# A hybrid pooling, SSD and gated-DeltaNet layer with mixture of experts: backward tokens stored reversed, inverses begun from 16-blocks and merged by matmuls

## The chip, the cores and the metric

The kernel runs on one core of one Trainium2 chip. A core has a matrix engine (PE, with its weight loads PEld), a vector engine (DVE), a scalar engine (ACT), a general engine (POOL) and a queue engine that issues transfers (SP). Each works through its own list of instructions in order, and they meet through semaphores. The metric is device microseconds of one execution, the median over runs.

## The reference

The program is one layer of a diffusion backbone over 2048 latent tokens and 256 context tokens of 1024 channels. After a modulated norm, one projection feeds three head groups: pooling, a bidirectional SSD scan and a bidirectional gated DeltaNet (GDN) scan. An output projection, a router and a mixture of 16 experts follow. The change is in GDN, which has 6 heads of 64 channels and works in chunks of 64 tokens, 36 chunks in each direction:

```python
def gdn_chunked(q, k, v, g, beta, s0):
    ...
    decay = jnp.exp(jnp.where(lower, gc[..., :, None] - gc[..., None, :], -jnp.inf))
    kb = kc * bc[..., None]
    xm = jnp.where(strict, jnp.einsum('bnhik,bnhjk->bnhij', kb, kc) * decay, 0.0)
    tm = lax.linalg.triangular_solve(xm + eye, jnp.broadcast_to(eye, xm.shape), ...)
    u = jnp.einsum('bnhij,bnhjv->bnhiv', tm, vc * bc[..., None])
    w = jnp.einsum('bnhij,bnhjk->bnhik', tm, kb * jnp.exp(gc)[..., None])
    attn = jnp.einsum('bnhik,bnhjk->bnhij', qc, kc) * decay
    ...
    def step(s, inp):
        v_new = u_i - jnp.einsum('bhlk,bhkv->bhlv', w_i, s)
        o_i = jnp.einsum('bhlk,bhkv->bhlv', qg_i, s) + jnp.einsum('bhij,bhjv->bhiv', a_i, v_new)
        s = s * ge_i[..., None, None] + jnp.einsum('bhlk,bhlv->bhkv', ke_i, v_new)
        return s, o_i
```

The backward direction is the same on tokens flipped in time, and its output is flipped back and added before a norm and a gate.

## The kernel before

The program has phases. **A** (lines 169 to 591) projects all tokens; `conv_block` also convolves blocks of 128 channels and writes them to DRAM, queries and keys by channel in `qk_d` (line 468), keys and values by token in `kv_d` (line 495). **Scalars** (593 to 781) makes the decay rows. **B** (790 to 1355) holds the scans. **C** (1361 to 1481) is the output projection and the router, **D** and **E** are the experts.

Phase B is where the change lies. A Python loop (line 1270) emits, for each step n, `gdn_prep(n)`, the SSD tiles of that step, `NINV` pieces of the batched inverses, then the recurrence `gdn_chain(nxt)`, which follows `LAG` steps behind, and from time to time two tiles of the output projection that need pooling and SSD alone (`fill_0`, "fills" below). The emitted order is not the executed one: a scheduler orders each engine's list by the priorities that `tc.high_priority` gives (the chain has the highest), and by the buffers of the pools.

- `gdn_prep(n)` multiplies keys by keys and queries for the chunk of both directions (lines 1019 and 1022). Forward and backward lie in one token order, so each direction's stationary operand `kz` is loaded apart, with zeros in the other half of its 128 rows (lines 1008 to 1010). DVE scales the products by the decay into `xk` and `XQ` (line 1025). `XQ` is written to `xq_d` (line 1027) and read again by `gdn_kv` (line 995). ACT copies the diagonal 32-blocks into a batch of 32 (line 1043).
- `gdn_inv(b)` inverts 32 blocks of 32x32 in each group of 32 partitions by forward substitution: 31 columns, two DVE operations each (lines 1071 and 1073), between transposes (1064, 1065, 1079 to 1082). `merge(n)` makes the 64-block inverse of a step from two 32-blocks in two rounds of matmuls (lines 1092 and 1093, then 1098 and 1099) with ACT copies between them.
- `gdn_chain(n)` is the recurrence: state times keys (line 1133), residual `gR` (1135), inverse times residual (1151), `vn` (1153, 1154), update (1159), new state `gS` (1163); for latent steps also the output from the state (1144) and from `vn` (1169). `gdn_out` (1180) finishes a chunk when both directions have reached it.

An fp32 matmul of the source is two MATMUL instructions in the trace, so the 12 of six heads and two directions are 24. A matmul's tile of the array is written rows*columns, as 64*32.

Of the kernel before, what the change touches and what calls it, by code (L numbers as in the profile page):

```python
# [42 lines left out]
FSR = P + H * P  # L43
RB = 1
HPO = 2000
NXQ = 2
SF = 0.9
LAG = 9
NINV = 7
NEND = 1  # L50
NPS = 3
# [19 lines left out]
def tile_kernel(ctx, tc, a, out, stop=None, dump=None):  # L71
# [34 lines left out]
    def rsqrt_newton(eng, y, x, tmp, n):  # L106
        """y = x ** -0.5 on [P, w] tiles (y and tmp F32)"""
# [6 lines left out]
    def rsqrt_bits(pool, x, shape, eng, name):  # L114
        """x ** -0.5 from the exponent's halving and Newton's iteration"""
# [21 lines left out]
    # ---------------------------------------------------------------- constants  # L137
# [7 lines left out]
    # ---------------------------------------------------------------- DRAM scratch  # L145
# [4 lines left out]
    qk_d = dram("qk_d", [6, P, TT])  # L150
    kv_d = dram("kv_d", [TT, 2 * HW])
    xb_d = dram("xb_d", [TT, HW + 256])
# [4 lines left out]
    gx_d = dram("gx_d", [216, P])  # L157
# [3 lines left out]
    xq_d = dram("xq_d", [NSTEP - CSTEP, P, HW])  # L161
# [6 lines left out]
    # ---------------------------------------------------------------- phase A: projections  # L168
# [10 lines left out]

    stA = ExitStack()  # L180
# [5 lines left out]
    def low(k, lo, hi):  # L186
        """low parts of hT's tokens lo .. hi - 1"""
# [9 lines left out]
    with tc.tile_pool(name="t1", bufs=1, side="right") as pool:  # L197
# [8 lines left out]
        # the modulation's weights lie where hT comes to lie, the first tokens where its last low parts do  # L206
# [10 lines left out]
        def raw_T(tiles):  # L217
            """the normed tokens of two tiles, transposed"""
# [96 lines left out]
        # rows of the small products that give the exponents: two of each head's, then those of the free tokens;  # L315
        # what of them is the same for all steps
# [75 lines left out]
        for r in range(2):  # L392
            S.dma_start(dap(ab_d, (TC + r) * 24, [[ROWS * 24, GW], [48, NT], [1, 24]]), ab[r * 64:(r + 1) * 64, NCT:, :])

# [18 lines left out]
    def proj(w, n):  # L413
        """block n of tokens: 0..3 lat, 4 ctx"""
# [26 lines left out]
    def conv_block(kind, cb):  # L441
        """kind 'q' (columns of qkv, column-major tokens) or 'x' (xbc)"""
# [12 lines left out]
        for n in (4, 0, 1, 2, 3):  # L455
# [11 lines left out]
            if kind == "q" and cb < 6:  # L467
                SY.dma_start(dap(qk_d, cb * P * TT + tok0, [[TT, P], [1, w]]), av)
# [32 lines left out]
    def ada_chunks(n):  # L501
        """128 columns at a time of m2 .. m5"""
# [69 lines left out]
    for blk in BLOCKS.split():  # L572
# [4 lines left out]
        if blk == "q6":  # L577
# [3 lines left out]
            for t, c in ((lnk, 0), (ssq, 6)):  # L581
                SY.dma_start(dap(ss_d, c, [[12, P], [P * 12, 18], [1, 6]]), t)
        conv_block(kind, cb)
        ada_chunks(2)
# [8 lines left out]
    # ---------------------------------------------------------------- scalars of the scans  # L593
# [21 lines left out]
    with tc.tile_pool(name="scal", bufs=1, side="right", reuse_waits="tile") as sp:  # L615
# [11 lines left out]
        def halves(name, lo, hi, anti=False):  # L627
# [3 lines left out]
            c0, c1 = (64, 0) if anti else (0, 64)  # L631
            V.tensor_copy(m[0:64, c0:c0 + 64], lo[0:64, 0:64])
            V.tensor_copy(m[64:128, c1:c1 + 64], hi[64:128, 64:128])
            return m

        g_inc = halves("g_inc", m_ge, m_le)
        g_str = halves("g_str", m_lt, m_gt)
        g_all = halves("g_all", ones, ones, anti=True)
# [24 lines left out]
        for h, d in ((0, 1), (64, 0)):  # L663
# [10 lines left out]
        # log(1 + e) = log(u) * e / (u - 1), or e where u is 1  # L674
# [10 lines left out]
        def put_rows(src, n, puts):  # L685
            """DRAM rows of 128 tokens from the n * 108 columns of src"""
# [15 lines left out]
        # GDN  # L702
# [31 lines left out]
        put_rows(fl(g2[:, 0]), 2, lambda t: SY.dma_start(dap(gx_d, 0, [[P, 108], [108 * P, 2], [1, P]]), t))  # L734
# [4 lines left out]
        # SSD  # L739
# [50 lines left out]
    # ---------------------------------------------------------------- phase B: scans  # L790
# [16 lines left out]
    SY.dma_start(dsk, dap(a["ssd_d"], 0, [[0, P], [1, 6]]))  # L807
    identb = gt_("identb", [P, P], 1, BF)
    V.tensor_copy(identb, ident)
    # NEG where the scan's order forbids a pair of tokens  # L810
# [18 lines left out]
    # rows 32-95 add NEG to the pairs that the order forbids  # L829
    for g in gPQt:  # L830
        for r in (slice(32, 64), slice(64, 96)):
            for s in range(2):
                V.tensor_scalar(g[r, s, 0:64], jp[r, 0:64], -32.0, NEG, op0=OP.is_lt, op1=OP.mult)
# [4 lines left out]
    # ---- SSD  # L838
# [97 lines left out]
    # ---- GDN: in token-major tiles rows 0-63 are the backward scan's chunk, rows 64-127 the forward scan's;  # L936
    # in channel-major tiles and in the state it is the other way round
# [860 lines left out]
```

## Time and profile before

| | us |
|---|---|
| runs, median of 3 (lowest to highest) | 2398.49 (2390.59 to 2404.88) |
| profiled execution: span from its first to its last instruction (no other time of it is given) | 2391.4 |
| busy in it: PE, DVE, ACT, POOL | 2084.4, 1733.0, 1077.5, 834.8 |
| phase B, from 782 to 1460 | 678 |

The busy time of an engine is the time in which at least one of its instructions ran; PE's matmuls overlap, so sums over groups of lines exceed it. The granted clock is the share of TensorE's full clock that it had over a stretch. The DMA share is the mean busy share of the 16 transfer engines.

### The profile page before, as it was taken

Reading aid. Unit: us, or ns where it says so; the run is one execution under the profiler, and the core shown is the slowest. Engines: PE = TensorE matmul, PEld = TensorE weight load, DVE = VectorE, ACT = ScalarE, POOL = GpSimd, SP = SyncE. Lnnn points to the kernel's source line nnn. Section 1 sums busy time; section 2 is a strip of 40 time slices with the busy share of each in tenths; the row PEclk is TensorE's granted clock in tenths of the full one; section 3 lists DMA queues with packets and bytes.
Section 4 is the critical chain, followed back from the end, with each engine's and each line's share of the span. In section 5 each row is a group of like instructions: output and inputs, shape, how many; then the busy total and the mean of one; then the engine's idle time right before and its main releaser. Section 6 shows DMA issues by size and latency. Waiting matters only on the chain. (4 is left out here: it accounts for less than half of the span.)

```text
span 2391.4 us, 44610 instructions
## 1 busy us (share of the span) xinstructions
PE 2084.4 (87%) x16769; PEld 1797.7 (75%) x16769; DVE 1733.0 (72%) x3635; ACT 1077.5 (45%) x2136; POOL 834.8 (35%) x755
## 2 busy tenths in 40 slices
PE   5789999999988667999988797996499999988886
PEld 2778888888867556778777676884489999978775
DVE  7666776877754698998898765546656766788876
ACT  5443333443314345556654442554144444455552
POOL 1002333355331435454453442445221111133453
PEclk8899999999989778999997898998699999998998
DMA  7433234433323997999876675655268778788883
GB/s 236 123 92 97 80 116 122 135 102 94 94 66 80 233 245 188 217 217 221 191 191 165 163 179 192 209 199 182 84 193 243 218 227 229 222 268 284 293 272 141
DMA packets 418033, 424.72 MB, mean 178 GB/s; under 512 B 151987, under 2 KB 312602, under 8 KB 416794
## 3 DMA queue, kind: packets, MB, share of 16 engines
q1 hardware_dynamic: 398106, 368.33, 53.6%
q0 software_dynamic: 14816, 50.03, 8.0%
q10 hardware_dynamic: 4896, 3.51, 0.5%
q8 instruction: 133, 2.18, 0.4%
q14 instruction: 82, 0.67, 0.1%
HBM read 309.55 MB, written 112.22 MB: 176 GB/s over the span
## 5 line engine op out<-in xcount | busy, mean ns | idle before, releaser
L1641 ACT ACTIVATE wh<-wr 128x1024 fp32r<-128x1024 f32 x192 | 202.1, 1056 | 255.5 <-PE pgate L134 74.7
L133 PE MATMUL pj<-hTh,wh 128*128 128x512 f32 (+1 forms) x800 | 308.1, 385 | 5.3 <-ACT wh L192 4.4
L461 DVE SCALAR_TENSOR_TENSOR acc<-u,PV,acc 128x512 f32<-128x512 f32 (+1 forms) x320 | 281.9, 930 | 39.1 <-ACT acc L459 21.1
L135 PE MATMUL pj<-hTh,wl 128*128 128x512 f32 (+1 forms) x800 | 306.9, 384 | 3.5 <-DVE wl L193 3.5
L134 PE MATMUL pj<-hTl,wh 128*128 128x512 f32 (+1 forms) x800 | 309.0, 386 | 0.0
L1643 DVE TENSOR_TENSOR wl<-wr,wh 128x1024 fp32r<-128x1024 f32 x176 | 221.3, 1263 | 104.8 <-ACT wh L1641 101.4
L133 PEld LDWEIGHTS pj<-hTh,wh 128*128 128x128 f32 x800 | 153.7, 192 | 37.4 <-ACT wh L192 4.7
L135 PEld LDWEIGHTS pj<-hTh,wl 128*128 128x128 f32 x800 | 153.3, 192 | 34.5 <-DVE wl L193 4.2
L134 PEld LDWEIGHTS pj<-hTl,wh 128*128 128x128 f32 x800 | 153.4, 192 | 29.6 <-issue 0.7
L506 POOL TENSOR_TENSOR aw<-aw,sc 128x1024 f32<-128x1024 f32 x32 | 68.4, 2139 | 251.1 <-DMA aw<-in_ada_w_dram 233.0
L134 PE MATMUL pgate<-xel,wh 128*128 128x256 f32 x512 | 151.0, 295 | 3.0 <-DVE xel L193 3.0
L133 PE MATMUL pgate<-xeh,wh 128*128 128x256 f32 x512 | 149.3, 292 | 3.6 <-ACT xeh L192 3.5
L135 PE MATMUL pgate<-xeh,wl 128*128 128x256 f32 x512 | 150.3, 294 | 0.0
L133 PE MATMUL pup<-xeh,wh 128*128 128x256 f32 x512 | 148.6, 290 | 0.0
L135 PE MATMUL pup<-xeh,wl 128*128 128x256 f32 x512 | 146.9, 287 | 0.0
L134 PE MATMUL pup<-xel,wh 128*128 128x256 f32 x512 | 146.7, 287 | 0.0
L1740 POOL DMA_INDIRECT x_d<-ye,idx x30 | 48.9, 1631 | 206.0 <-DVE ye L1734 128.6
L1071 DVE TENSOR_TENSOR tmpb<-Wb,Vb 128x31 f32<-128x31 f32 (+15 forms) x217 | 107.7, 496 | 5.7 <-POOL Vb L1063 1.9
L1073 DVE TENSOR_TENSOR Vb<-Vb,tmpb 128x31 f32<-128x31 f32 (+15 forms) x217 | 108.7, 501 | 3.7
L133 PE MATMUL pdown<-wh,hh 128*128 128x512 f32 x256 | 104.6, 408 | 7.6 <-DVE ye L1734 3.3
L133 PEld LDWEIGHTS pgate<-xeh,wh 128*128 128x128 f32 x512 | 101.4, 198 | 5.0 <-ACT xeh L192 4.6
L134 PEld LDWEIGHTS pgate<-xel,wh 128*128 128x128 f32 x512 | 101.6, 198 | 3.2 <-DVE xel L193 3.2
(581 smaller groups left out, 5927.8 us busy)
## 6 DMA issues: line engine op xcount, KB each, us to landing
wr<-in_exp_w_gate_dram SPq DMA_DIRECT2D x64, 512.0 KB
wr<-in_exp_w_up_dram SPq DMA_DIRECT2D x64, 512.0 KB
wr<-in_exp_w_down_dram SPq DMA_DIRECT2D x64, 512.0 KB
aw<-in_ada_w_dram SPq DMA_DIRECT2D x32, 512.0 KB
kv<-kv_d SPq DMA_DIRECT2D x72, 192.0 KB
xb<-xb_d SPq DMA_DIRECT2D x35, 320.0 KB
wr<-in_w_in_dram SPq DMA_DIRECT2D x21, 512.0 KB
aw<-in_ada_w_dram SPq DMA_DIRECT2D x8, 1024.0 KB
```

The costliest lines, as they stand in the source:

```text
L133: TE.matmul(o, lh, rh, start=start, stop=False, **kw)
L134: TE.matmul(o, lh, rl, start=False, stop=False, **kw)
L135: TE.matmul(o, ll, rh, start=False, stop=stop, **kw)
L461: V.scalar_tensor_tensor(av, u[:, s0 - 2 + i:s0 - 2 + i + w], cw[:, i, cb:cb + 1], av, op0=OP.mult, op1=OP.add)
L506: G.tensor_tensor(w, w, sc2[:, :, 0:1].to_broadcast([P, KT, P]), op=OP.mult)
L1071: V.tensor_tensor(t, W[:, c + 1:, c:c + 1].to_broadcast([P, nr, ncl]), N[:, c:c + 1, :ncl].to_broadcast([P, nr, ncl]), op=OP.mult)
L1073: V.tensor_tensor(N[:, c + 1:, :ncl], N[:, c + 1:, :ncl], t, op=OP.subtract)
L1641: S.activation(wh, w, AF.Copy)
L1643: (G if nw[0] <= 16 else V).tensor_tensor(wl, w, wh.bitcast(F32), op=OP.subtract)
L1740: G.indirect_dma_start(out=x2_d, out_offset=rows_of(e, h), in_=ys[h], in_offset=None, compute_op=OP.bypass if late else OP.add)
```

## The change

Backward tokens are stored in reversed order, so that both directions have the same lower-triangular form: rows 0 to 63 of every tile are the forward scan, rows 64 to 127 the backward one. Then:

- `qk_d` gets one 6 KB row for a channel, a pair of chunks and a direction, written twice by `conv_block`, the second time from a copy that ACT reverses. Copies of `kv_d`, `ab_d` and `ss_d` with reversed tokens are made by DRAM-to-DRAM transfers (`reverse`).
- The matmuls of prep and chain contract 64 rows, and the two directions alternate; `kz` and its zeros are gone. Query products stay in `xk` (9 buffers) and do not go through `xq_d`. `vn` and `gS` are one operation for both directions in place of two.
- Inverses start from 16-blocks: 15 columns of at most 128 elements in place of 31 of at most 256. `merge` makes 32-blocks and then 64-blocks in five rounds of matmuls, three of them in 32*32 tiles.
- `gdn_out` turns and adds the other direction's output by a matmul with `turned`, `go_d` is written in chunks and read by four transfers in place of one.
- `LAG` 9 to 7, `NINV` 7 to 6, PSUM banks of SSD (`NPS`) 3 to 2, of `pm` 1 to 2.

```diff
+QKR = 2 * H * P
-LAG = 9
-NINV = 7
+LAG = 7
+NINV = 6
-NPS = 3
+NPS = 2
...
+    def reverse(dst, src, w, c, n):
+        for k0, k in ((CSTEP, NSTEP - CSTEP), (0, CSTEP)):
+            o = k0 * 64 * w + c
+            SY.dma_start(dap(dst, o, [[64 * w, k], [w, 64], [1, n]]), dap(src, o + 63 * w, [[64 * w, k], [-w, 64], [1, n]]))
...
             if kind == "q" and cb < 6:
-                SY.dma_start(dap(qk_d, cb * P * TT + tok0, [[TT, P], [1, w]]), av)
+                rv = ct("st", 512, 3)
+                S.activation(rv[:, :w], av[:, ::-1], AF.Copy)
+                for src, m in ((av, t0), (rv[:, :w], 18 + (0 if n == 4 else NSTEP // 2 + CSTEP // 2 - t0 - nt))):
+                    for h in range(2):
+                        SY.dma_start(dap(qk_d, m * 64 * QKR + (1 - cb // 3) * H * P + (2 * (cb % 3) + h) * P,
+                                         [[QKR, 64], [64 * QKR, nt], [1, P]]), src[64 * h:64 * h + 64])
...
     def load_kq(m, name, bufs):
-        n = 2 * m
-        kq = (gt_ if name == "kq" else lt)(name, [P, 2, H, 2, HD], bufs)
-        for i in range(2 if n >= CSTEP else 1):
-            o = (0 if i else HW) * TT
-            SY.dma_start(kq[0:64, i].rearrange("p h s t -> p h (s t)"),
-                         dap(qk_d, o + n * 64, [[TT, 64], [64 * TT, H], [1, P]]))
-            for s in range(2):
-                SY.dma_start(kq[64:128, i, :, s, :], dap(qk_d, o + chunk_b(n + s) * 64, [[TT, 64], [64 * TT, H], [1, 64]]))
+        kq = (gt_ if name == "kq" else lt)(name, [P, 2, H, P], bufs)
+        for d in range(2):
+            SY.dma_start(kq[DS[d]].rearrange("p a b c -> p (a b c)"),
+                         dap(qk_d, (18 * d + m) * 64 * QKR, [[QKR, 64], [1, QKR]]))
         return kq
...
-            for i in range(3):
-                h = 3 * hg + i
-                TE.matmul(pg[64:128, i, 0:nq, :], kz[:, 0, h, :], kq[:, 0:nq, h, s, :], start=True, stop=True)
             for i in range(3):
                 h = 3 * hg + i
-                TE.matmul(pg[0:64, i, 0:nq, :], kz[:, 1, h, :], kq[:, 0:nq, h, s, :], start=True, stop=True)
+                for d in range(2):
+                    TE.matmul(pg[DS[d], i, 0:nq, :], of(kq, d, 0, h, s), of(kq, d, slice(0, nq), h, s), start=True,
+                              stop=True)
...
         def column(c):
-            W, N = T_["W"], T_["N"]
-            nr, ncl = 31 - c, c + 1
+            W, N = diagonal(T_["W"]), diagonal(T_["N"])
+            nr, ncl = 15 - c, c + 1
...
             for h in range(h0, h1):
-                c = n * H + S0 + h - 32 * b
-                TE.matmul(pm[96:128, 0, h, :], xo[64:128, h, :], yt[64:128, c, :], start=True, stop=True)
-                TE.matmul(pm[0:32, 0, h, :], xo[0:64, h, :], yt[0:64, c, :], start=True, stop=True)
-            for p0 in (96, 0):
-                S.activation(qt[p0:p0 + 32, h0:h1], pm[p0:p0 + 32, 0, h0:h1], AF.Copy)
+                for q in range(4):
+                    c = 32 * (q % 2)
+                    TE.matmul(pa[QS[q], h, :], xk[QS[q], h, 0, c:c + 32], yt[QS[q], c0 + h, 0:16], start=True, stop=True)
+            V.scalar_tensor_tensor(a16[:, hh, 0:16], pa[:, hh, :], upper[:, 0:1],
+                                   eyes[:, 0:1, 0:16].to_broadcast([P, w, 16]), op0=OP.mult, op1=OP.add)
             for h in range(h0, h1):
...
+                for q in range(4):
+                    TE.matmul(py[QS[q], 0, h, :], a16[QS[q], h, :], yd[QS[q], c0 + h, :], start=True, stop=True)
+            for h in range(h0, h1):
+                for q in range(4):
+                    TE.matmul(py[QS[q], 1, h, :], yd[QS[q], c0 + h, :], a16[QS[q], h, :], start=True, stop=True)
...
+            for h in range(h0, h1):
+                for d in range(2):
+                    TE.matmul(pm[DS[d], 0, h, :], xk[QS[2 * d], h, 0, :], y2[QS[2 * d], 1, h, :], start=True, stop=True)
+            S.activation(a32[:, hh, 0:32], pm[:, 0, hh, :], AF.Copy, scale=-1.0)
...
             ks = bank(pb, "pc", [H, HD], 1)
-            for d, (o, i) in enumerate(fb):
-                for h in range(H):
-                    TE.matmul(ks[o, h, :], kqg[:, 0, h, s, :], st[:, d, h, :], start=True, stop=True)
+            for h, d in hd:
+                TE.matmul(ks[DS[d], h, :], of(kqg, d, 0, h, s), st[DS[d], h, :], start=True, stop=True)
...
-        V.tensor_tensor(h3(oe), po, h3(oe), op=OP.add)
+        TE.matmul(po.rearrange("p h d -> p (h d)"), turned, oe, start=False, stop=True, skip_group_check=True)
```

The order of the lists shows three of its places. On PE, around one late step of the recurrence; names are tiles, `pc` the chain's bank, `pm` the merges' bank, `pp` prep's, and a row gives the line, the tiles and the moving operand's shape. Before:

```order
L1005 MATMUL pp<-gPQ_6141 128x384
L1019 MATMUL pp<-kq,kz_6202 64x128 x3
L1133 MATMUL pc<-gS_6225,kqg 64x64 x12
L1144 MATMUL po<-gS_6225,kqg 64x64 x12
...
L1151 MATMUL pc<-gR,Yt_6207 64x64 x12
L1022 MATMUL pp<-kq,kz_6202 64x128
...
L1092 MATMUL pm<-YT,XO_6189 32x32
L1093 MATMUL pm<-YT,XO_6189 32x32
```

and in the change:

```order
L1177 MATMUL pc<-gR,Yt_6367 64x64 x12
L947 MATMUL ps<-xb,sE 128x64 x5
L1121 MATMUL pm<-YT,xk 32x16 x9
L1183 MATMUL pc<-vn,ke 64x64 x12
L1191 MATMUL po<-vn,xk 64x64 x12
L1207 MATMUL po<-oe_13850,turned 128x384
L1121 MATMUL pm<-YT,xk 32x16 x4
L1167 MATMUL pc<-gS,kqg 64x64 x12
```

A merge's rounds are now cut into pieces that stand between the chain's groups, and every change of the tile's shape is one more. Counted over phase B, from the first `gPQ` matmul to the last output of `vn`, the shape changes 416 times before and 782 times now, and the source's matmuls go from 4058 to 6649.

On DVE, the last columns of a batch of inverses (`tmpb` is the product, `Vb` the inverse) before:

```order
L1071 TENSOR_TENSOR tmpb<-Wb,Vb 128x112
L1073 TENSOR_TENSOR Vb<-Vb,tmpb 128x4x28
L1071 TENSOR_TENSOR tmpb<-Wb,Vb 128x87
```

and in the change:

```order
L1095 TENSOR_TENSOR tmpb<-Wb,Vb 128x110
L1097 TENSOR_TENSOR Vb<-Vb,tmpb 128x2x5x11
L1095 TENSOR_TENSOR tmpb<-Wb,Vb 128x96
L886 TENSOR_TENSOR S_7759<-ssg,ps 128x384
L1097 TENSOR_TENSOR Vb<-Vb,tmpb 128x2x4x12
```

Each column still has two operations, on two 16-blocks at once, and a batch has 15 columns.

On SP, the loads of a pair of steps before (`kz`, the products' round trip, and rows of 64 and 128 tokens):

```order
L966 DMA kqg<-qk_d 64x6x64 x2
L963 DMA kqg<-qk_d 64x6x128
L966 DMA kqg<-qk_d 64x6x64 x2
L991 DMA kv<-kv_d 64x768
L1010 DMA kz_6202<-qk_d 64x6x64
...
L1027 DMA xq_d<-XQ 128x384
```

and in the change:

```order
L1030 DMA kv<-kvr_d 64x768
L1004 DMA kq<-qk_d 64x1536 x2
L1217 DMA go_d<-oe 64x384 x2
```

Six issues for the keys and queries of a pair have become two, and `kz`, `xq_d` and `XQr` have gone.

## Rows read from the trace of the kernel before

**Rows 1.** Busy time by stretch: length, PE, PEld, DVE, ACT, POOL; clock, DMA share, GB/s.
```profile
300.00:400.00 100.00, 100.00 (x521) 84.14 (x520) 68.29 (x93) 37.20 (x57) 36.28 (x28) 1.00 0.42 124
782.00:876.00 94.00, 58.11 (x390) 45.41 (x390) 71.49 (x135) 38.82 (x105) 40.35 (x54) 0.70 1.00 246
1000.00:1200.00 200.00, 184.12 (x2651) 158.95 (x2653) 179.37 (x357) 122.69 (x358) 96.53 (x103) 0.95 0.89 210
1200.00:1460.00 260.00, 217.26 (x3023) 190.34 (x3023) 198.80 (x431) 118.54 (x357) 116.96 (x179) 0.89 0.66 170
1500.00:1600.00 100.00, 100.00 (x593) 82.69 (x592) 49.34 (x153) 50.41 (x127) 47.43 (x20) 1.00 0.56 196
```

**Rows 2.** The same view over the whole of phase B.
```profile
782.00:1460.00 678.00, 566.72 (x7596) 487.68 (x7596) 563.01 (x1148) 351.85 (x1028) 308.32 (x394) 0.89 0.81 199
```

**Rows 3.** Groups of PE's instructions in phase B: busy us, mean ns, idle before.
```profile
L1019 PE MATMUL pp<-kq,kz 128*64 128x128 f32 (+1 forms) x432 | 64.2, 297 | 7.2 <-ACT gE L1007 3.9 <-PE pp L1005 1.7 <-DMA kq<-qk_d 0.6
L1169 PE MATMUL po<-vn,XQr 128*64 128x64 f32 x768 | 56.7, 230 | 1.6 <-ACT vn L1153 1.4
L1159 PE MATMUL pc<-vn,ke 128*64 128x64 f32 x840 | 50.5, 229 | 0.9 <-ACT vn L1154 0.9
L907 PE MATMUL ps<-S,cb 128*128 128x192 f32 x64 | 14.0, 344 | 0.0
```

**Rows 4.** Timeline of PE: start us, us, line, tiles, tile shape, count, wait.
```profile
1100.25 0.19 PE L1098 MATMUL pm<-Yd,Qt 64*32 64x32 f32 x1
1100.26 0.19 PE L1099 MATMUL pm<-Yd,Qt 64*32 64x32 f32 x1
1100.28 0.19 PE L1098 MATMUL pm<-Yd,Qt 64*32 64x32 f32 x1
1100.29 0.19 PE L1099 MATMUL pm<-Yd,Qt 64*32 64x32 f32 x1
1100.41 0.65 PE L1019 MATMUL pp<-kq,kz 128*64 128x128 f32 x4
...
1108.12 1.43 PE L1144 MATMUL po<-gS,kqg 128*64 128x64 f32 x24 [2.45 <-DVE fx L1226]
1109.49 1.43 PE L1151 MATMUL pc<-gR,Yt 64*64 64x64 f32 x24
```

**Rows 5.** Groups of DVE's instructions in phase B, as in rows 3.
```profile
L1073 DVE TENSOR_TENSOR Vb<-Vb,tmpb 128x31 f32<-128x31 f32 (+15 forms) x217 | 108.7, 501 | 3.7
L1071 DVE TENSOR_TENSOR tmpb<-Wb,Vb 128x31 f32<-128x31 f32 (+15 forms) x217 | 107.7, 496 | 5.7 <-POOL Vb L1063 1.9
L1163 DVE TENSOR_TENSOR gS<-gSG,pc 64x384 f32<-64x384 f32 x68 | 37.4, 550 | 13.8 <-PE pc L1159 12.7
L1080 DVE STREAM_TRANSPOSE Yd<-Vb 64x1024 f32<-64x1024 f32 x7 | 14.3, 2042 | 0.2
```

**Rows 6.** Single lines: durations ns min/median/max, first and last start us.
```profile
L1133 PE MATMUL pc<-gS,kqg x840: 219/222/369, 888.1 to 1448.4; 128*64 128x64 f32 x168
L1064 DVE STREAM_TRANSPOSE Wb<-Db x7: 1904/1955/2000, 815.9 to 1263.1; 64x1024 f32<-64x1024 f32 x7
L932 PE MATMUL ps<-ident,sy x48: 271/273/476, 952.1 to 1450.1; 128*128 128x128 f32 x48
```

**Rows 7.** Transfers in phase B: packets and sizes, and issues with KB each.
```profile
DMA packets 199244, 134.73 MB, mean 199 GB/s; under 512 B 117937, under 2 KB 178345, under 8 KB 199150
...
kz<-qk_d SPq DMA_DIRECT2D x72, 96.0 KB
xq_d<-XQ SPq DMA_DIRECT2D x32, 192.0 KB
```

**Rows 8.** Single lines of phase A, as in rows 6.
```profile
L468 SPq DMA_DIRECT2D qk_d<-acc x30: 319/332/383, 382.5 to 566.9; - x30
L464 ACT ACTIVATE acc<-acc x45: 398/632/646, 382.0 to 653.9; 128x512 f32<-128x512 f32 x36, 128x256 f32<-128x256 f32 x9
```

More of the change, by code (lines that the diff above doesn't have):

```diff
@@ L1101, in merge @@
-            S.activation(y[32:64, h0:h1, 0:32], pm[32:64, 1, h0:h1], AF.Copy, scale=-1.0)
-            for g4 in range(4):
-                c = 32 * (g4 % 2)
-                ps = slice(32 * g4, 32 * g4 + 32)
-                S.activation(y[ps, h0:h1, c:c + 32], yd[ps, c0:c0 + w, :], AF.Copy)
+            c0 = n * H + S0 - 32 * b
+            assert n - NY not in YM
+            y, xk, a16, a32 = Yt[n % NY], XK[n], A16[n % 2], A32[n % 2]
+            hh = slice(h0, h1)
+            w = h1 - h0
@@ new lines, in merge @@
+            pm = bank(pb, "pm", [2, H, 32], 2)
+            for h in range(h0, h1):
+                for d in range(2):
+                    TE.matmul(pm[DS[d], 0, h, :], xk[QS[2 * d], h, 0, :], y2[QS[2 * d], 1, h, :], start=True, stop=True)
+            S.activation(a32[:, hh, 0:32], pm[:, 0, hh, :], AF.Copy, scale=-1.0)
+            for h in range(h0, h1):
+                for d in range(2):
+                    TE.matmul(pm[DS[d], 1, h, :], a32[QS[2 * d + 1], h, :], y2[QS[2 * d + 1], 0, h, :], start=True,
+                              stop=True)
@@ L1106, in merge @@
+            S.activation(y[:, hh, 32:64], pm[:, 1, hh, :], AF.Copy)
             if h1 == H:
                 YM[n] = y
-                XO.pop(n)
         steps = range(max(0, 32 * b - S0) // H, min(NSTEP, (32 * b + 31 - S0) // H + 1))
-        return ([begin] + [lambda c=c: column(c) for c in range(31)] + [end], [lambda n=n: merge(n) for n in steps])
+        return ([begin] + [lambda c=c: column(c) for c in range(15)] + [end], [lambda n=n: merge(n) for n in steps])
     ST = [None]
@@ L1146, in gdn_chain @@
         pvn = bank(pb, "pc", [H, HD], 1)
-        with tc.issue_after(last.ins) if lat else nullcontext():
-            for d, (o, i) in enumerate(fb):
-                for h in range(H):
-                    TE.matmul(pvn[o, h, :], y[o, h, :], R[o, h, :], start=True, stop=True)
-        vn = vnt[n % 2]
-        S.activation(vn[64:128, 0], pvn[64:128], AF.Copy)
-        S.activation(vn[0:64, 1], pvn[0:64], AF.Copy)
+        for h, d in hd:
+            TE.matmul(pvn[DS[d], h, :], y[DS[d], h, :], R[DS[d], h, :], start=True, stop=True)
@@ L1166, in gdn_chain @@
-        if lat:
-            for d, (o, i) in enumerate(fb):
-                for h in range(H):
-                    TE.matmul(po[o if early else i, h, :], xq[:, h, :], vn[:, d, h, :], start=False, stop=True,
-                              skip_group_check=True)
-            if early:
+            for h, d in hd:
+                TE.matmul(pu[DS[d], h, :], ke[DS[d], h, :], vn[DS[d], h, :], start=True, stop=True)
+            ST[0] = lt("gS", [P, H, HD], 2)
+            if n:
+                V.tensor_tensor(ST[0], sg, pu, op=OP.add)
+            else:
+                V.tensor_copy(ST[0], pu)
@@ L1172, in gdn_chain @@
+        if lat:
+            for h, d in hd:
+                TE.matmul(po[DS[d], h, :], xk[DS[d], h, 1, :], vn[DS[d], h, :], start=False, stop=True,
+                          skip_group_check=True)
+            l = n - CSTEP
+            if l < 16:
                 oe = lt("oe", [P, HW], 1)
```

240 lines of the change are left out of this document (117 added, 123 removed).

## The prediction

> **What bounds the kernel now.** I read the busy time by stretch first. Outside phase B PE is busy all the time at full clock (two sample stretches, [rows 1]), so there only PE's work counts, and the change adds none of it. Phase B is different: over its 678 us PE is busy 567 us, DVE 563 us, and the transfer engines 0.81 of it, at a mean clock of 0.89 [rows 2]. Three resources are nearly level, and by stretch the limit moves. In the first 94 us the transfers are full (share 1.00) while PE is busy only 58 us at a clock of 0.70; from 1000 to 1200 PE has 92% and DVE 90%; from 1200 on PE has 84% [rows 1].
>
> The view of single lines gives the pace. The recurrence's first state product starts at 888 and its last at 1448 [rows 6]: 35 of them, 16.5 us apart. A step's own chain is far shorter: three groups of matmuls of 1.4 us [rows 4] and the DVE and ACT operations between them, some 7 us. So a step waits mostly in PE's and DVE's lists, behind SSD, prep, merges and inverses. What takes work from those lists shortens phase B; PE, as the fullest, sets how far.
>
> **The change, part by part.** PE in phase B, from 567 us:
>
> *Chain.* A group of 24 instructions takes 1.43 us, 0.053 apart with 0.22 us for the last [rows 3, 4, 6]. They stand one direction after the other, in one lane. Now the directions alternate in two tiles of 64*64. That tiles overlap is in the trace: L1098 and L1099 read different halves of the rows and write different partitions of one bank, and start 0.01 us apart, 0.03 a pair [rows 4]. So a group takes 12 x 0.053 + 0.22 = 0.83 us and saves 0.60. There are five such groups in a step, x768 to x840 (first and last in [rows 3]), about 170 bursts: 102 us at full clock, 115 at 0.89. Lower bound: nothing, if they do not overlap.
>
> The Trainium skill has a rule against this, in "TensorEngine Tiling (Array Packing)", section "Gotcha 1: PSUM Pressure": different row tiles cannot access the same PSUM bank simultaneously. By that rule this term would be 0 in place of 115. The pair above does write one bank `pm` from two row tiles, 0.01 us apart, so the trace disagrees for two tiles; for four no run here shows it.
>
> *Prep.* Four instructions of 128 columns take 0.65 us, 0.11 apart [rows 4], in runs of three or six in one lane; 24 a step. Alternating halves 2.6 us to 1.3, in 34 steps' worth (four context steps count half): 44 us. The runs overlap a little at their seams now, so I take 40.
>
> *Merges.* Now two rounds of 24 in two lanes: each 12 x 0.03, so 0.72 us a step, 26 us. After: three rounds of 48 in four lanes and two of 24 in two lanes. If four lanes run side by side, each round is again 12 x 0.03 = 0.36: 1.8 us a step, 65 us. That is +39, or +44 at the mean clock. From below it could be +0, if 16 columns go quicker than 32 and rounds hide under others; from above all 192 instructions follow each other at 0.03, 5.8 us a step, 207 us. I take 44, the value nearest to the row of two lanes.
>
> *Changes of tile shape.* From L1099 to L1019, in another shape, PE takes 0.12 us with no wait shown, against 0.03 for a pair within one shape [rows 4]; so a change costs about 0.09. The order counts 416 before and 782 now: +33 us.
>
> *Turning* of `oe`: 16 matmuls of 384 columns, each two instructions; by the 0.34 us of L907 for 192 columns [rows 3], pipelined 0.3 us each: +10.
>
> Sum for PE: 567 - 115 - 40 + 44 + 33 + 10 = **499 us**.
>
> DVE: the columns are 217 + 217 operations, 216 us [rows 5]; now 210 of at most 128 elements, where the mean form has about 160: at 0.4 us, 84. Seven batches had six transposes of 2 us, now three: -42. One state operation in place of two: -18. Scaling and `oe`: about -20. 563 falls to some 350 us. The merges' new step on DVE (40 of about 0.3 us) is in that. ACT and POOL stay at or under half busy: merges lose copies and gain four a step.
>
> Transfers: `kz` (72 x 96 KB) and the round trip through `xq_d` (2 x 32 x 192 KB), together 19 MB of 135, go away, and most of the 117,937 packets under 512 B become 6 KB rows [rows 7]. So the full first 94 us get lighter. There the first batch of inverses also stands in the way: it begins at 816, and the chain's first state product comes 72 us later [rows 6]; 62 column operations at 0.5 us are 31 of them. With 30 of 0.4 and half the transposes that is 12 + 6, and the chain starts some 40 us sooner.
>
> *New waits.* A merge now has three returns of ACT or DVE to PE in place of one. What is queued behind the waiting matmul on PE is the chain's next group or SSD's, as the order shows; the cover is that the rounds are cut apart and other work stands between. SSD has two PSUM banks in place of three (a rival below). Prep may run nine steps ahead of the chain, by `xk`'s buffers.
>
> PE's idle time in phase B is now 111 us: 36 in the first 94, 16 in 200 (8%) where lists are full, 43 in 260 later [rows 1]. With the earlier start I take 20, and 10% of the rest, 50: 70 us. So phase B is 499 + 70 = 569, **109 less**.
>
> Phase A: 30 reversed copies on ACT of 0.63 us [rows 8] are 19 us on an engine that is busy 37%, under a PE busy all the time [rows 1]. Each copy takes one of three `st` buffers until its two transfers land, and there are four SP issues of 0.33 us [rows 8] where there was one; three more, 1 us in 30 places, is 30 us if all of it reached PE. `pj` has three banks of about 5 us of PE, so I take **+5**, with 0 and 30 as ends. If that cover went, ACT would hold PE's banks. The `reverse` transfers wait on SP for the writes they copy; behind them are weight loads, which are a block ahead. In phase C three more issues a tile lie under PE's 100%: 0; without that cover the first tile would be about 1 us late.
>
> Sum: 2391.4 - 109 + 5 = 2287 against the profiled execution's span. The runs' median, 2398.5, is 7 above that span, so the forecast is **2294 us**.
>
> **The rivals.**
>
> *PE was held by others.* If DVE at 350 us and lighter transfers let PE run as it does from 1000 to 1200 (clock 0.95, 8% idle [rows 1]), its 499 become 499 x 0.89/0.95 = 467, and phase B 508: 170 less, 2398.5 - 170 + 5 = **2234**. For it: the low clock of 0.70 belongs to the stretch that transfers fill. Against: merges bring more small gaps.
>
> *SSD holds the end.* L932 shows one SSD tile every 33 us, from 952 to 1450 [rows 6]. With two banks instead of three, that pace may stay: the first tile's end, 170 us into the phase, comes 40 sooner, 15 more tiles take 495, and 10 us follow: 635, 43 less, **2360**. Against it: those tiles are now filler behind the chain's priority.
>
> *Merges run in one lane*, the rival on the other side. If the four 32*32 tiles of a round do not overlap, the merges are 207 us instead of 65: +142, at 0.89 +160. Phase B is 729, 51 more than now: 2398.5 + 51 + 5 = **2454**. It decides from 65 + 104 x 0.89 = 158 us for 6912 instructions, 0.023 us each, where I count on 0.009 and one lane has 0.03. By the skill's rule above, the chain's 115 and prep's 40 would be missing too, and the time would be 2609; since the trace shows two lanes in one bank, I give that no chance of its own beyond this one's.
>
> **How the numbers follow.** Forecast 0.60, PE freed 0.18, SSD 0.14, one lane 0.08. The range reaches from below the second case, with room for its idle time, to above the third: **2200 to 2385**. About 0.5% (12 us) is what a measurement of this kernel can tell from no change. Faster: nearly all of the first three cases, 0.87; slower: 0.08; the rest, 0.05, is for bounds that cancel out (no overlap in the chain, 30 us in phase A).
>
> **What would show it.** The chain's groups should take about 0.85 us for 24 instructions, prep's 0.055 a matmul, rounds of merges 0.009 an instruction, and DVE's busy time in phase B fall by 200 us. Phase B should last 550 to 590 us, its first state product come about 60 to 70 us after its start, not 106. PE's busy time near 567 again, or merges' rounds of 48 taking over 1.1 us, would be the slower rival; L932 still 33 us apart at the phase's end, the SSD one. Phase A longer by more than 20 us, with ACT waiting for `st`, would prove my cover wrong.

## The result and the profile after

The changed kernel takes 2598.59 us (median of 4 runs, 2588.94 to 2604.25), the kernel before 2394.54 beside it: a ratio of 1.0858, 95% interval 1.0815 to 1.0902. I had forecast 2294, and gave "slower" a chance of 0.08. The profiled execution spans 2602.5 us, 211 more than before.

Nearly all of the loss lies in phase B. Its first gate matmul starts at 783.3 (782.4 before), so phase A is not longer, and of the 211 us only 10 fall behind the recurrence's end. The recurrence's state products (L1167) and SSD's tiles (L959), as in [rows 6]:

```profile
L1167 PE MATMUL pc<-gS,kqg x840: 218/218/366, 866.8 to 1649.3; 64*64 64x64 f32 x168
L959 PE MATMUL ps<-ident,sy x48: 272/374/477, 999.9 to 1529.2; 128*128 128x128 f32 x48
```

The chain starts 21 us sooner and ends 201 us later: a step takes 23 us (782.5 / 34) where it took 16.5. The view by stretch, with the columns of [rows 1]; the last row answers to [rows 2]:

```profile
782.00:866.00 84.00, 57.02 (x769) 44.36 (x769) 54.34 (x126) 26.80 (x68) 30.12 (x37) 0.70 0.87 237
1000.00:1200.00 200.00, 151.97 (x2761) 123.97 (x2761) 75.79 (x172) 62.80 (x181) 62.51 (x68) 0.76 0.49 125
...
782.00:1680.00 898.00, 701.03 (x12818) 565.74 (x12819) 372.73 (x855) 271.30 (x765) 264.73 (x347) 0.74 0.49 132
```

The relief I counted on is there: DVE 373 us where it had 563, the DMA share 0.49 for 0.81. Yet PE is busy 701 us in place of 567, idle 197 in place of 111, and its clock is 0.74. At full clock its work is nearly what it was: 567 x 0.89 is 504 us before, 701 x 0.74 is 519 after. So most of the 134 us that its busy time grew by is the lower clock. No engine is full, so the phase waits. For what, the waits from 882 on say, first of after, then of before (engine, operation, what it waited for: us, times, longest):

```profile
ACT eg L1021 <- DMA eg<-gx_d: 121.0, 14, 13.3
POOL ke L1158 <- PE pc L1183: 104.4, 19, 18.6
POOL kqg L1024 <- DMA kqg<-qk_d: 92.6, 11, 16.2
```

```profile
POOL sy L902 <- PE ps L932: 52.7, 7, 14.8
...
POOL kqg L985 <- DMA kqg<-qk_d: 35.0, 6, 12.0
...
ACT eg L983 <- DMA eg<-gx_d: 15.1, 4, 6.2
```

ACT stands 121 us at the exponential of `eg`, which it did for 15, POOL 93 at its multiply. One such wait in the timeline of after:

```profile
1184.17 3.56 POOL L1024 TENSOR_TENSOR kqg<-kqg,eg 128x768 f32<-128x768 f32 x2 [6.92 <-DMA kqg<-qk_d]
...
1187.76 1.09 SPq L1019 DMA_DIRECT2D eg<-gx_d  x2
...
1188.26 1.01 POOL L943 TENSOR_TENSOR sy<-sy,syi 128x384 f32<-128x384 f32 x1
...
1190.42 0.99 POOL L950 TENSOR_TENSOR sy<-sy,zt 128x384 f32<-128x384 f32 x1
1192.54 0.84 ACT L1021 ACTIVATE eg<-eg 128x768 f32<-128x768 f32 x1 [9.61 <-DMA eg<-gx_d]
1193.29 0.31 ACT L1137 ACTIVATE A<-pm 128x192 f32<-128x192 f32 x1
1193.50 0.51 ACT L952 ACTIVATE zt<-sy 128x384 f32<-128x384 f32 x1
...
1194.13 0.15 DVE L953 TENSOR_SCALAR sss<-sss 128x1 f32<-128x1 f32 x1 [5.75 <-ACT zt L952]
...
1196.54 0.87 PE L959 MATMUL ps<-ident,sy 128*128 128x128 f32 x3 [6.70 <-DVE sy L955]
```

`eg` has one buffer. POOL waits for `kqg`, multiplies, and only then SP issues the next `eg` (1187.76). ACT has been standing at its exponential since 1182.93. Behind that, in ACT's list, wait a merge's return (L1137) and SSD's `zt`, behind `zt` DVE, and behind DVE PE, 6.7 us. POOL's list has its part in this gap: SSD's L943, whose last operand ACT had finished at 1182.55, stands behind the multiply until 1188.26, so that `zt` has its operand only at 1191.41, and ACT lets it start at 1193.50. For the exponential itself POOL waited only twice in the whole run, 2.4 us. Before, ACT did other work between the issue of the same load and its exponential, which then found its data there:

```profile
1074.02 1.28 SPq L981 DMA_DIRECT2D eg<-gx_d  x2
...
1075.74 2.76 ACT L1105 ACTIVATE Yt<-Yd 32x64 f32<-32x64 f32 x10 [4.25 <-DVE Yd L1079]
...
1089.80 0.85 ACT L983 ACTIVATE eg<-eg 128x768 f32<-128x768 f32 x1
```

45 ACT instructions stand between the two. In after no ACT instruction stands there in 12 of 18 feeds; before in 3. Of the 121 us that ACT stands, 57 lie before the load is even issued, and the rest is the load's own time, 4 us or more each.

PE's clock around such a gap, in stretches of 4 us (PE busy, granted clock, DMA share, GB/s):

```profile
1180.00:1184.00 4.00, 2.46 (x35) 0.77 0.67 145
1184.00:1188.00 4.00, 4.00 (x53) 0.50 0.00 0
1188.00:1192.00 4.00, 1.84 (x92) 0.87 0.80 161
1192.00:1196.00 4.00, 0.00 (x0) 0.55 0.47 127
1196.00:1200.00 4.00, 3.46 (x34) 0.50 0.96 237
1200.00:1204.00 4.00, 4.00 (x27) 0.50 0.23 85
1204.00:1208.00 4.00, 4.00 (x42) 0.50 0.01 4
1208.00:1212.00 4.00, 4.00 (x79) 0.81 0.09 25
```

PE stands from 1189.8 to 1196.5, and then runs at half clock (1.2 GHz) until after 1208, though it is busy 11.5 of those 12 us. It is the second fall in these rows: the clock was already at half from 1184 to 1188, with PE busy throughout, after a gap of only 1.5 us (1181.1 to 1182.6).

The merges, as groups of PE's instructions from 782 to 1680 in after, and from 782 to 1460 before (columns of [rows 3]):

```profile
L1140 PE MATMUL pm<-y,A 32*64 32x32 f32 x864 | 55.2, 259 | 14.3 <-ACT A L1137 9.3 <-issue 5.0
L1136 PE MATMUL pm<-y,xk 32*64 32x32 f32 x864 | 53.8, 250 | 20.0 <-ACT Yt L1132 14.2 <-ACT y L1131 5.4 <-issue 0.3
...
L1129 PE MATMUL pm<-A,Yd 32*32 32x32 f32 x1728 | 37.6, 208 | 3.9 <-issue 3.9
L1126 PE MATMUL pm<-Yd,A 32*32 32x32 f32 x1728 | 36.5, 211 | 10.5 <-DVE A L1122 10.5
...
L1121 PE MATMUL pm<-YT,xk 32*32 32x16 f32 x1728 | 30.1, 194 | 3.7 <-DVE YT L1104 3.0 <-issue 0.7
```

```profile
L1092 PE MATMUL pm<-YT,XO 64*32 64x32 f32 x432 | 24.6, 198 | 10.5 <-DVE YT L1081 9.8 <-ACT Yt L1101 0.6
L1093 PE MATMUL pm<-YT,XO 64*32 64x32 f32 x432 | 24.5, 198 | 3.4 <-DVE YT L1082 3.4
L1099 PE MATMUL pm<-Yd,Qt 64*32 64x32 f32 x432 | 23.4, 200 | 0.0
L1098 PE MATMUL pm<-Yd,Qt 64*32 64x32 f32 x432 | 23.2, 200 | 6.3 <-ACT Qt L1095 6.3
```

Each group's busy time overlaps its neighbours'. If every instruction is given the time from its start to the next start (or to its own end, if that is sooner), the parts add up to PE's busy time; so counted, merges hold PE 181 us where they held 44, and the two rounds in 32*64 tiles 96 of them. The chain's five groups hold it 182 us (240 before), prep's matmuls 79 (84). With each part multiplied by the clock granted at its moment, that is at full clock 132 us for the merges (41 before), 134 for the chain (218) and 58 for prep (74).

### The profile page after: what moved, and what is told of

Same layout as the page of the kernel before. It is cut to its first block, busy times and chain, and to the rows that moved or that the text cites. A ratio compares the mean times of both kernels' runs of the same rounds, so it can differ in the third digit from the quotient of the medians.

```text
span 2602.5 us, 54175 instructions
## 1 busy us (share of the span) xinstructions
PE 2217.2 (85%) x21985; PEld 1874.6 (72%) x21985; DVE 1527.3 (59%) x3328; ACT 1011.5 (39%) x1898; POOL 778.1 (30%) x695
## 5 line engine op out<-in xcount | busy, mean ns | idle before, releaser
L469 DVE SCALAR_TENSOR_TENSOR acc<-u,PV,acc 128x512 f32<-128x512 f32 (+1 forms) x320 | 273.0, 900 | 53.8 <-ACT acc L467 36.1
L1669 DVE TENSOR_TENSOR wl<-wr,wh 128x1024 fp32r<-128x1024 f32 x176 | 228.3, 1303 | 100.6 <-ACT wh L1667 98.7
L135 PEld LDWEIGHTS pgate<-xeh,wl 128*128 128x128 f32 x512 | 102.7, 201 | 0.0
L135 PE MATMUL pdown<-wh,hl 128*128 128x512 f32 x256 | 101.8, 398 | 0.6 <-DVE hl L200 0.6
```

The costliest lines, as they stand in the source:

```text
L135: TE.matmul(o, ll, rh, start=False, stop=stop, **kw)
L469: V.scalar_tensor_tensor(av, u[:, s0 - 2 + i:s0 - 2 + i + w], cw[:, i, cb:cb + 1], av, op0=OP.mult, op1=OP.add)
L1669: (G if nw[0] <= 16 else V).tensor_tensor(wl, w, wh.bitcast(F32), op=OP.subtract)
```

## Experiments

Three theories: **feed** (the lists stand at the loads of `eg` and `kqg`), **work** (the merge rounds hold PE) and **lead** or **banks** (`LAG` and `NPS`, two small numbers of the change). Medians in us; ratios are to the kernel before beside them.

**e1: no feed.**

```diff
-        eg = lt("eg", [P, 2, H, HD], 1)
-        ... loads, exponential, multiply
-            V.tensor_tensor(R, v, ks, op=OP.subtract)
+            V.scalar_tensor_tensor(R, ks, 0.0, v, op0=OP.mult, op1=OP.add)
```

> Leaves out the feed's scaling: eg is neither loaded nor exponentiated, POOL does not multiply kqg, and R is v plus zero times the state product (same operands, same engine). Theory 'feed' (ACT and POOL stand in their lists at the loads of eg and kqg: 113 and 76 us in phase B, and SSD and the chain stand behind them): both waits go, phase B falls from 895 to 740-790 us, time 2450-2500. Theory 'banks' (SSD with two PSUM banks sets the pace): L959's tiles stay some 35 us apart, time 2580-2600. Theory 'work' (merge rounds and a PE with more, smaller instructions set the pace): PE stays at about 700 us attributed and the time within 20 us of 2599.

In `R` the state product now counts zero times. 2509.91, ratio 1.049 (1.0434 to 1.0546): 89 less than after, and 10 above what "feed" wanted. The feed's scaling has a price, less than half of the loss. The kernel before scales its feed too, and no run leaves it out there: the 89 us are the price of the scaling as it stands in the change, and what it cost before was not measured.

**e2: the exponential before storing.** `S.activation(t, t, AF.Exp)` in `put_gx`, none in `gdn_feed`.

> gx_d is exponentiated once in phase A/B's start before it is stored, so ACT has no operation on eg in the loop; POOL's multiply and all loads stay. Theory 'feed': ACT's 113 us of waits on eg go, POOL now waits for eg or kqg itself (76 us or more stay); about half of the feed's loss comes back, 2500-2560. Theories 'banks' and 'work': 18 ACT operations of about 0.8 us less, no change beyond 15 us: 2585-2600.

2540.79, ratio 1.0618 (1.058 to 1.0657), 58 less. POOL still waits 92.1 us for `kqg`. As "feed" said.

**e3: three banks for SSD.** `NPS = 3`, `pm` one bank.

> Three PSUM banks for SSD as before, one in place of two for the merges and fills (pm). Theory 'banks': SSD tiles come 30 us apart or less, DVE's wait for sEb (76 us) and PE's for sy (39 us) shrink, 2480-2540. Theory 'feed': the waits on eg and kqg stay, 2580-2620. Theory 'work': merges with one bank run one after the other, slower, 2600-2660.

2581.87, ratio 1.0814 (1.077 to 1.0859). SSD's tiles now come 28 us apart:

```profile
L959 PE MATMUL ps<-ident,sy x48: 272/417/476, 938.5 to 1361.2; 128*128 128x128 f32 x48
```

but the chain still ends at 1614.8. SSD does not hold the end, and "banks", which wanted 2480 to 2540, falls. What the merges lose by their one bank in this run is not separated.

**e4: the small numbers alone, in the kernel before.** `LAG = 7`, `NPS = 2`.

> The kernel before with the two small parameters of the change alone: LAG 7 in place of 9 and NPS 2 in place of 3. Theory 'banks' (or a shorter lead of the prep): most of the loss appears here without the rest of the change, 2450-2550. Theories 'feed' and 'work': 2390-2420, within 1% of before.

2438.28, ratio 1.0201 (1.0164 to 1.0238): 45 us, less than "banks" wanted, more than the others. A shorter lead and one bank less have a price of their own; the two were not tried apart.

**e5, e9, e10: the last two rounds.** All three stand on e1. e5 leaves them out; e9 keeps one head of six and every copy; e10 keeps all instructions and takes the returns away.

For e9, in both rounds, and for e10, in the operands of L1136 and of L1140:

```diff
-            for h in range(h0, h1):
+            for h in range(h0, h0 + 1):
...
-                    TE.matmul(..., xk[QS[2 * d], h, 0, :], y2[QS[2 * d], 1, h, :], ...)
+                    TE.matmul(..., xk[QS[2 * d], h, 0, :], yd[QS[2 * d], c0 + h, :], ...)
...
-                    TE.matmul(..., a32[QS[2 * d + 1], h, :], y2[QS[2 * d + 1], 0, h, :], ...)
+                    TE.matmul(..., xk[QS[2 * d + 1], h, 0, :], yd[QS[2 * d + 1], c0 + h, :], ...)
```

> As e1_nofeed, and the last two rounds of every merge (L1136 and L1140, 1728 instructions, and the ACT copy between them) are left out; the lower half of y is a copy of the round before. In e1 PE's time between their starts and the next was 85 us, at a clock of 0.80. Theory 'work' (merge rounds hold PE): at least 60 us less than e1's 2510, 2420-2450, and the clock of phase B near 0.85 or more. Theory 'lead' (what is left of the loss after the feed comes from the shorter lead of prep and SSD's two banks): within 25 us of e1, 2485-2510.

> As e1_nofeed, but the last two rounds of a merge are made for one head in place of six (the copies of ACT between and behind them stay, of one head's result spread over six). Both returns of ACT to PE, the two changes of tile shape and the waits are as in e1; of 1728 instructions some 170 stay. e5_trim, without the rounds, gained 116 us over e1. Theory 'rounds are PE time' (instructions of 32 rows and 64 columns, 0.03 us apart at full clock and 0.05 at half): nearly all of the 116 comes back, 2395-2430. Theory 'rounds are returns' (PE stands behind ACT's copies): less than a third, 2475-2510.

> As e1_nofeed, with all instructions of the last two rounds, but with operands that are there already (yd in place of y2, xk in place of a32), so that no matmul waits for a copy of ACT inside these two rounds. Theory 'rounds are PE time': within 30 us of e1, 2480-2515. Theory 'rounds are returns': most of the 116 us comes back, 2395-2430.

e5 2393.7 (1.0011, 0.999 to 1.0032), e9 2393.69 (1.0022, 1.0005 to 1.004), e10 2486.74 (1.041, 1.0373 to 1.0446). With the returns but without the instructions the whole 116 us come back; with the instructions but without the returns 23. So it is the instructions of these rounds that cost, not the returns. From 782 to the chain's end PE's clock goes from 0.78 to 0.84, first e1, then e9:

```profile
782.00:1548.00 766.00, 647.36 (x12630) 527.31 (x12632) 344.79 (x822) 253.55 (x731) 198.16 (x247) 0.78 0.52 140
```

```profile
782.00:1441.00 659.00, 557.74 (x11276) 448.59 (x11280) 344.01 (x822) 251.53 (x730) 197.90 (x247) 0.84 0.61 163
```

The stretch is 107 us shorter, 90 of them PE's busy time; PE's idle time, 119 and 101 us, changes little. At full clock PE's work falls by less than half of that, from 647 x 0.78 = 505 us to 558 x 0.84 = 469; the clock gives the rest. Nor do gaps alone make the clock: at the same busy share, 92%, it was 0.96 in before and 0.79 in e1, with more and smaller instructions. What lowers it there no run separates.

```profile
1082.00:1182.00 100.00, 91.77 (x1333) 79.64 (x1332) 88.92 (x165) 59.96 (x177) 47.22 (x50) 0.96 0.92 212
```

```profile
1182.00:1282.00 100.00, 92.00 (x1681) 75.09 (x1674) 42.77 (x104) 36.21 (x106) 30.68 (x38) 0.79 0.51 137
```

**e6: `LAG = 8`** (seven `Y` tiles; `gR`, `vn`, `gSG` one buffer).

> The change with LAG 8 in place of 7 (seven Y tiles; gR, vn and gSG with one buffer each to make room, which the chain's own order covers). Theory 'lead': with LAG 9 to 7 and NPS 3 to 2 worth 45 us in e4, one step back gives 10-25 us, 2570-2590. Theories 'feed' and 'work': within 10 us of 2599.

2592.49 (1.0849, 1.0831 to 1.0867), 6 less and within the intervals, where "lead" wanted 10 to 25: one step back in the lead shows nothing while the feed and the rounds stand.

**e7, e8, e13: why ACT stands at `eg`.** e7: `eg` two buffers (`gR`, `vn` one). e8: exponential and multiply in a `gdn_scale(m)` of their own, called one chain step later. e13: `eg` in pieces of 256 bytes:

```diff
-            SY.dma_start(eg[DS[d]].rearrange("p a b c -> p (a b c)"),
-                         dap(gx_d, (2 * m + d) * H * P, [[0, 64], [1, H * P]]))
+            for q in range(2):
+                SY.dma_start(eg[DS[d], q], dap(gx_d, (2 * m + d) * H * P + HD * q, [[0, 64], [2 * HD, H], [1, HD]]))
```

> The change with two buffers of eg (gR and vn with one, to make room), so that SP issues its loads without waiting for POOL's last multiply. Theory 'feed, late issue': ACT's wait for eg falls from 113 us to under 40, 2530-2560, like e2. Theory 'feed, early place in ACT's list' (the order puts the exponential right behind its own load whenever that is issued): the wait stays above 80 us, 2580-2610.

> The loads of kqg and eg stay where they are; the exponential and POOL's multiply are asked for one chain step later, behind the chain step that runs in between. Theory 'feed': the waits on eg and kqg fall below 60 us together (from 190), 2510-2550. Theory 'work' or 'lead': 2585-2610. Slower than 2610 if the scaling now comes too late for the chain's own state product.

> The change, with eg alone loaded in pieces of 256 bytes again (gx_d stored by head; four issues of SP a feed in place of two, 768 pieces each two); the bytes, the buffers and the program's order of calls are the change's. Theory 'place in the list' (the order puts the exponential where it believes the load to have landed; with rows of 6 KB it believes that it lands at once): the exponential now stands some 5 or more ACT operations behind its issue, as before, where there were none in 12 of 18 feeds, and ACT's wait for eg falls from 113 us to under 60; time 2540-2590. Theory 'the transfer itself' (what costs is the load's own length): the wait grows, 2600-2640.

2600.51 (1.0886, 1.0857 to 1.0914), 2621.79 (1.0974, 1.0953 to 1.0994) and 2582.48 (1.0808, 1.0757 to 1.0858). ACT's waits for `eg` from 882 on, in this order:

```profile
ACT eg L1021 <- DMA eg<-gx_d: 113.9, 14, 13.1
```

```profile
ACT eg L1025 <- DMA eg<-gx_d: 115.6, 15, 13.8
```

```profile
ACT eg L1022 <- DMA eg<-gx_d: 91.6, 13, 13.9
```

A second buffer leaves the wait, but it did not bring the load forward either. SP still issues it right behind one of POOL's multiplies, and waits there nearly as long, first after, then e7:

```profile
SPq L1019 <- POOL kqg L1024: 82.1, 11, 10.7
```

```profile
SPq L1019 <- POOL kqg L1024: 78.3, 11, 10.8
```

Half of ACT's wait, 57 us, lies before the issue in e7 as in after (1 us in the kernel before). So e7 does not rule the late issue out. Asking one step later leaves the wait as it is, and the time is 23 us worse. Smaller pieces take a quarter of it off: "the transfer itself" wanted more, "place in the list" less than 60 us, and in 8 of 18 feeds still no ACT instruction stands between; its time is within the intervals of after. What is seen is that ACT stands at the exponential before its load is issued, and that the issue stands behind POOL's multiply; what moved the exponential there is not settled.

**e11, e12, e14, e15, e18: repairs.** All stand on e2 and compute all that after computes. e11: 31 columns again (`NINV = 7`), rounds one to three gone. e12: the other two rounds in 32*32 tiles. e14, e15: e11 and e12 with `LAG = 9`, `NPS = 3`. e18: e15 with `kq` and `kqg` loaded by halves.

```diff
-            W, N = diagonal(T_["W"]), diagonal(T_["N"])
-            nr, ncl = 15 - c, c + 1
+            W, N = square(T_["W"]), square(T_["N"])
+            nr, ncl = 31 - c, c + 1
...
-                    TE.matmul(pm[DS[d], 0, h, :], xk[QS[2 * d], h, 0, :], ...)
+                    TE.matmul(pm[QS[2 * d + 1], 0, h, :], xk[QS[2 * d], h, 0, 32:64], ...)
```

The first pair is e11's, the second e12's.

> A version that should compute the same: as e2_expd, but the inverse goes by 31 columns of 32-blocks on DVE as before (NINV 7), so that the first three rounds of each merge (5184 instructions of four lanes, 84 us of PE's time in the change) and one return fall away; the last two rounds stay as they are. DVE, busy 25 to 54% of phase B in the change, gets some 130 us back. Theory 'work' (PE's merges): 2541 minus 70 to 110, 2430-2470. Theory 'DVE was rightly relieved': DVE's columns hold the merges again, 2530 or more.

> As e11_cols32, and the last two rounds in tiles of 32*32 in place of 32*64 (only the quarter that is read is computed; the other half of y's columns is copied by ACT, two more operations of ACT and three copies in halves). Theory 'work, priced by tile shape': tiles of 32*32 cost half of 32*64 or less, so of the 116 us of e5 another 40 to 80 come back: 2350-2410. Theory 'returns': within 15 us of e11_cols32.

> As e11_cols32, with the lead and banks of before: LAG 9, NPS 3 (merges and fills with one bank pm), seven Y tiles; room from A16, gR, vn and gSG. Theory 'lead' (45 us in e4): 2385-2415. Theory 'work': within 15 us of e11, 2420-2450.

> As e14_cols32_lead, with e12's rounds in 32*32 tiles. If PE's time and the lead both hold the phase: 2350-2390, which would beat both kernels; if only the lead: like e14, 2385-2415.

> As e15_cols32_q_lead, with kq and kqg loaded by halves (keys, then queries, rows of 3 KB; in the context's two pairs of steps the keys alone, as before the change). Theory 'feed': POOL's wait for kqg (63 us in e15) falls below 45 and the time to 2380-2398, at or just under before. Theory 'no more to be had there': 2395-2412.

| | us | ratio, 95% interval |
|---|---|---|
| e11 | 2435.72 | 1.0211 (1.0171 to 1.025) |
| e12 | 2434.1 | 1.0176 (1.015 to 1.0201) |
| e14 | 2444.93 | 1.0224 (1.0177 to 1.0272) |
| e15 | 2403.62 | 1.0052 (1.003 to 1.0074) |
| e18 | 2394.52 | 1.0019 (1.0003 to 1.0036) |

Rounds one to three, against the columns, cost 105 us (e2 to e11). Smaller tiles (e12) or the old lead (e14) alone give nothing, both together 32 us. So in e12 "work, priced by tile shape" missed (it wanted 2350 to 2410), and in e14 "lead" (2385 to 2415). To the chain's end, first e11, then e12:

```profile
782.00:1492.00 710.00, 557.94 (x7524) 458.58 (x7526) 478.45 (x1016) 237.72 (x700) 265.10 (x281) 0.78 0.62 164
```

```profile
782.00:1490.00 708.00, 532.09 (x7589) 432.41 (x7591) 473.74 (x1017) 282.27 (x859) 264.96 (x281) 0.78 0.61 163
```

PE's busy time falls by 26 us, the stretch by 2: idle time took its place. But e12 also adds copies on ACT, which is busy 282 us in place of 238; what the tiles give without these copies was not tried. In e18 POOL's wait for `kqg` is 48.7 us ("feed" wanted under 45), and the time is within 0.4% of the kernel before. No version that computes everything beats it.

**e16, e17: the savings without their price.** No feed, 31 columns, the last rounds for one head; e17 also with the old `LAG` and `NPS`.

> All that the change saves, and little of what it adds: e1's feed without eg, columns of 32 on DVE as before (NINV 7), and the last two rounds for one head of six, so that PE's merges almost disappear. It says what my forecast's savings (115 of the chain, 40 of the prep, 109 for the phase in all) are worth without their price. If they are as sized: 2240-2310. If the savings themselves were oversized (the chain's and prep's instructions run at half clock in more of the phase): 2320-2400.

> As e16_no_added, with LAG 9, NPS 3, one pm bank and seven Y tiles as in e14. PE's idle time in phase B of e16 was 161 us, where my forecast had 70. Theory 'lead' (the short lead and two banks make that idle time): 30 to 50 us less than 2347, 2295-2320, near the forecast. Theory 'list order' (idle time grows as PE's work falls, whatever the lead): 2335-2360.

2347.01 (0.9825, 0.978 to 0.987) and 2314.24 (0.969, 0.9656 to 0.9724). The stretch to the chain's end in e17:

```profile
782.00:1366.00 584.00, 466.59 (x6084) 379.58 (x6085) 453.63 (x1015) 234.53 (x700) 203.79 (x247) 0.83 0.70 187
```

PE is idle 117 us even with nearly no merges in the way. The 76 us by which e17 beats the kernel before are not the savings alone: that kernel scales its feed, and its own merges hold PE 44 us, and e17 leaves out the scaling and five heads of six. Read upwards, the runs are a ladder from best case to change (the kernel before beside them took 2389 to 2395):

| step | us | adds |
|---|---|---|
| before | 2390 | |
| e17, no scaling, one head of six in the last rounds | 2314 | -76 |
| e16, shorter lead, fewer banks | 2347 | +33 |
| e9, columns of 16 and rounds one to three | 2394 | +47 |
| e1, last two rounds whole | 2510 | +116 |
| after, the feed's scaling | 2599 | +89 |

A step's price depends on what stands below it: rounds one to three were 47 here and 105 from e2 to e11.

## Why the prediction was wrong

What failed is the sum for phase B. Its 499 + 70 us of PE's work and idle time came out as 701 + 197 (782 to 1680), because the clock fell, the merges were priced by another tile's row, idle time did not shrink, and the feed and the lead were put at nothing.

*Clock: kept at 0.89.* By it the 499 us are 444 at full clock. Measured are 519, 75 more. At 0.89 these 519 would be 583 us; at 0.74 they took 701. So 118 us are the clock alone, more than the 84 us (at 0.89) of work that the forecast missed. That "merges bring more small gaps" stood in my text, without a price.

*Chain and prep: right by the group, not in the phase.* I had 0.83 us for a group of 24 (its own terms, 12 x 0.053 + 0.22, give 0.86). In the timeline of after it takes 0.92 (0.87 at best), but 1.54 at half clock, more than the 1.43 of before [rows 4]. Prep's 12 take 0.87, some 0.055 apart, with the same reservation. In the phase, by the count above, the chain's -115 came to -58 and prep's -40 to -5; at full clock the chain saved 84 of 102 us, prep 16 of 40. The groups, one by one:

```profile
1162.22 0.87 PE L1050 MATMUL pp<-kq 64*64 64x128 f32 x12
1163.75 0.59 PE L1121 MATMUL pm<-YT,xk 32*32 32x16 f32 x48
...
1347.26 1.54 PE L1177 MATMUL pc<-gR,Yt 64*64 64x64 f32 x24
1354.20 0.92 PE L1167 MATMUL pc<-gS,kqg 64*64 64x64 f32 x24
...
1395.12 0.89 PE L1140 MATMUL pm<-y,A 32*64 32x32 f32 x24
```

*Merges: the term "+44" failed.* The lanes were right: 48 instructions in 32*32 tiles take 0.59 us (1163.75), so the rival "Merges run in one lane" names the wrong mechanism. (By the Trainium skill, "TensorEngine Tiling (Array Packing)", section "Gotcha 1: PSUM Pressure", different row tiles cannot access one bank at once. The trace disagrees: in the row at 1163.75 four of them write one bank `pm` in turn, 0.01 us apart.) But I gave the two rounds of 24 the 64*32 tile's 0.03 a pair, 0.36 a round; a round in 32*64 tiles takes 0.89 (1395.12), nearly as long as a chain group of 64*64, and 0.67 of it from the first start to the last. That makes 36 x 2 x 0.67 = 48 us where I had 26, at full clock. Cut into pieces between other work, and partly at half clock, the five rounds came to the 181 us above, where I had some 44 + 44; at full clock to 132, where I had 65. That is still short of the 158 us (at full clock too) from which, by my own rival, the change loses: its side came true, but neither by its mechanism nor by the merges alone. The +33 for changes of tile shape was not tried apart.

*Idle time: "10% of the rest" failed, and with it the sum.* I took PE as the bound and let its idle time fall to 70 us as DVE and the transfers were relieved. It rose to 197; e17, with next to none of the added work, still has 117 in 584. With less to do PE still waits for the other lists, and its clock in e17 is 0.83, not above the 0.89 of before.

*Feed: costed at nothing.* The loads became fewer and larger, as I wrote; "ACT and POOL stay at or under half busy" was no cover. A list stands still at its first waiting operation, however idle its engine: ACT, busy 271 of 898 us, stood 121 at `eg`. Without the scaling 89 us come back (e1), without the exponential in the loop 58 (e2).

*Lead: costed at nothing.* `LAG` had no price; the fewer banks stood among the rivals, for SSD. Together with the banks it is 33 us (e17 to e16) and 45 in the kernel before (e4), 30 from e12 to e15, but nothing from e11 to e14.

*Right:* DVE's 190 us, phase A (1 us later), the chain's sooner start in its sign (83 us after 783.3, where I had 60 to 70). "SSD holds the end" was wrong: e3. One reading was too wide: behind phase B, from 1460 to the end, PE of the kernel before is busy 812 of 931 us at a clock of 0.93, not all the time at full clock.

## What to carry to other kernels

When no engine is full, ask what each list stands at, and who is behind it: an operation that follows its own load directly stops all work behind it, even on an engine at 30%. Price a new tile shape by a row of that very shape, and do not carry the old clock over into a phase with more gaps and smaller instructions: here the clock alone lengthened PE's work by 118 us. Before a structure with more rounds replaces work on another engine, measure it with the rest held still: here the best case was 76 us, with some of the old work left out as well, and what came on top cost 285.

## What the runs showed of the hardware

- A 32*64 tile with 32 columns costs nearly as much as a 64*64 tile with 64: at full clock 24 take 0.89 us beside 0.92. In e12 a round in 32*32 tiles takes 0.57 for 24:

```profile
1356.51 0.57 PE L1120 MATMUL pm<-YT,xk 32*32 32x32 f32 x24
```

- Four row tiles of 32*32 run side by side into one bank: 48 instructions of 16 columns in 0.59 us.
- After 6.7 us without a matmul PE ran 12 us at half clock, though busy for 11.5 of them; and after 1.5 us without one it ran from 1184 to 1188 at half clock, busy throughout. With PE busy 92% of 100 us the granted clock was 0.96 in one stretch and 0.79 in another.
- The share of the transfer engines fell from 0.81 to 0.49 in a kernel that became 8.6% slower. What the lighter transfers gave by themselves no run separates; in the phase's first stretch the share went from 1.00 to 0.87, and the chain started 21 us sooner.
